# Log-sum-exp of 16,384 rows: one row's exponentials on GpSimd as powers of e, summed on VectorE ahead of the fifth load

## The chip, the cores and the metric

The kernel runs on one core of a Trainium2 chip. The metric is the device time of one execution in microseconds (us). Three runs of the kernel before the change gave 162.43, 162.54 and 162.83 us. One further execution was taken with the hardware profiler.

The core's engines work at the same time and wait for each other by semaphores. ScalarE (ACT in the profile) computes exponentials and logarithms, VectorE (DVE) sums, GpSimd (POOL) so far sets a few constants, TensorE (PE) does one tiny product at the end. SyncE (SP) issues the transfers, which 16 DMA engines carry out.

## The reference

The input is 32 x 512 rows of 1024 float32 numbers, 67.1 MB; of each row the logarithm of the sum of its exponentials is wanted.

```python
def reference(x, axis):
    x_max = np.max(x, axis=axis, keepdims=True)
    return (x_max.squeeze(axis) + np.log(np.sum(np.exp(x - x_max), axis=axis))).astype(np.float32)
```

## The kernel before

Each of the 128 partitions owns 128 rows that follow each other in memory, so "one row" below means one row in every partition: 128 x 1024 numbers, 0.52 MB. The kernel does not subtract the maximum. It takes exp(x) directly, sums, takes the logarithm, and then tests that all the sums lie between 1e-18 and 1e18. If they don't, a second pass (lines 189 to 201 and 322 to 343) reads everything again and subtracts the maxima. With the numbers at hand the first pass suffices.

The rows come in 17 loads, the list `CHUNKS` (line 10). An entry has the rows of the load, how many of them VectorE sums, in how many parts those are worked, and whether VectorE sums "by halves". The loads have 4, 15, 16, 16, 16, 14, 13, 9, 7, 5, 4, 3, 2, 1, 1, 1, 1 rows. They go into a ring of 51 row slots in the on-chip memory (`ring`, line 75); lines 118 to 125 give each load its slots one behind the other, and start again at slot 0 where a load doesn't fit any more.

Per load the code (lines 213 to 270) does this:

- SyncE issues the load (line 155), once the sums and exponentials of the rows that lay in its slots before are done. `busy` (line 128) holds for each slot the number of VectorE's or ScalarE's instruction to wait for. SyncE issues in order: a load that waits holds up the loads behind it. The first load is moved ahead of the opening barrier (lines 352 to 360).
- ScalarE waits for the landing (line 233) and writes the exponentials over the rows, one instruction for each part (line 235). For a load of `(16, 15, 2, False)` the parts have 8 and 7 rows; `cuts` (line 131) gives the first part the larger half.
- VectorE waits for each part (line 239) and sums its rows: one reduction for the part (line 255), or, by halves, one instruction a row that adds the row's halves and accumulates (line 242, with a read of the accumulator behind it).
- The rows beyond the second number of the entry are left to ScalarE alone: exponential and sum in one instruction (line 262, with a read of the accumulator behind it).

Everything on an engine runs in the order of the code. The logarithms are on ScalarE: of the first 81 rows ahead of the eighth load (line 219), of the next 43 ahead of the last load's exponential (line 221), of the last four at the end (line 272). The second of these waits for VectorE's sums of the thirteenth load, and the last row's exponential (line 225) is queued behind it. Then VectorE takes the largest and smallest of 124 sums (lines 293 and 294), compares with the bounds (line 283, twice), TensorE counts (lines 304 and 307), VectorE sums the counts (line 312), and the engines branch on the result.

GpSimd's only work is to set the bounds and the weights of that count (lines 206 to 209); the last of its settings raises `pool_done`, for which VectorE waits at line 298.

Of the kernel before, what the change touches and what calls it, by code (L numbers as in the profile page):

```python
# [1 line left out]

# [5 lines left out]


CHUNKS = [  # L10
# [4 lines left out]
]  # L15

CUTS = ()
RING_ROWS = 51


UNEVEN = ()
# [17 lines left out]
def kernel(  # L39
# [6 lines left out]
    nc = tc.nc  # L46
    P = nc.NUM_PARTITIONS
# [4 lines left out]
    N, D = x_flat.shape  # L52
# [5 lines left out]
    fp32, bf16, int32 = mybir.dt.float32, mybir.dt.bfloat16, mybir.dt.int32  # L58
    Exp = mybir.ActivationFunctionType.Exp
    Ln = mybir.ActivationFunctionType.Ln  # L60
    Alu = mybir.AluOpType
    AX = mybir.AxisListType.X
# [11 lines left out]

    ring = nc.alloc_sbuf_tensor("ring", [P, RING_ROWS, D], fp32).ap()
    sums = nc.alloc_sbuf_tensor("sums", [P, NB], fp32).ap()
# [4 lines left out]
    weights = nc.alloc_sbuf_tensor("weights", [P, 2], bf16).ap()  # L81
    verdict = nc.alloc_sbuf_tensor("verdict", [1, 1], int32).ap()
    peak = nc.alloc_sbuf_tensor("peak", [P, NB], fp32).ap()
    votes = nc.alloc_psum_tensor("votes", [P, 512], fp32).ap()
    late = nc.alloc_psum_tensor("late", [P, 512], fp32).ap()

# [4 lines left out]
    landed = [nc.alloc_semaphore(f"landed{i}") for i in range(len(CHUNKS) + len(spans) - 1)]  # L91
    act_done = nc.alloc_semaphore("act_done")
    dve_done = nc.alloc_semaphore("dve_done")
    pool_done = nc.alloc_semaphore("pool_done")
# [20 lines left out]
    symbolic, nc._always_lower_symbolic_ap = nc._always_lower_symbolic_ap, False  # L115


    place = []
    row = slot = 0
    for r, *_ in CHUNKS:  # L120
        if slot + r > RING_ROWS:
            slot = 0
        place.append((slot, row))
        slot += r
        row += r


    busy = [(0, 0)] * RING_ROWS
    acts = dves = 0

    def cuts(n, parts):
        ends = [-(-n * k // parts) for k in range(parts + 1)]
        return [(lo, hi) for lo, hi in zip(ends, ends[1:]) if lo < hi]

    def load(i):
        (s, row), r = place[i], CHUNKS[i][0]
        act_wait = max(a for a, _ in busy[s : s + r])
        dve_wait = max(d for _, d in busy[s : s + r])
        if dve_wait:
            nc.sync.wait_ge(dve_done, dve_wait)  # L140
        if act_wait:
            nc.sync.wait_ge(act_done, act_wait)
        dst, src = ring[:, s : s + r], x_v[:, row : row + r]
        if i == len(CHUNKS) - 1:
            for k, (lo, hi) in enumerate(spans):
                nc.sync.dma_start(out=dst[:, :, lo:hi], in_=src[:, :, lo:hi]).then_inc(
                    landed[i + k], 16
                )
        elif i in UNEVEN:
            for first, last, step in PARTS:  # L150
                nc.sync.dma_start(
                    out=dst[first:last:step], in_=src[first:last:step]
                ).then_inc(landed[i], 16)
        else:
            nc.sync.dma_start(out=dst, in_=src).then_inc(landed[i], 16)

    def take_logs(lo, hi, src, dve_wait, act_wait, bias=0.0):
        nonlocal acts
        nc.scalar.wait_ge(act_done, act_wait)
        if dve_wait:  # L160
            nc.scalar.wait_ge(dve_done, dve_wait)
        nc.scalar.activation(out=res[:, lo:hi], in_=src, func=Ln, bias=bias).then_inc(  # L162
            act_done, 1
        )
        acts += 1
# [4 lines left out]
    def total(t):  # L170
        return late[:, t - late_row : t - late_row + 1] if t >= late_row else sums[:, t : t + 1]
# [17 lines left out]
    with nc.body("second_vector", valid_engines=vector):  # L189
        for k, (lo, hi) in enumerate(steps):  # L190
# [5 lines left out]
                out=part, in0=part, in1=peak[:, lo:hi].unsqueeze(2).to_broadcast([P, hi - lo, D])  # L196
# [6 lines left out]
    nc.switch_bb("first_pass")  # L203

    nc.scalar.preload_act_table_set("natural_log_exp_and_others")  # L205
    nc.gpsimd.memset(bounds[:, 0], LOW)  # L206
    nc.gpsimd.memset(bounds[:, 1], HIGH)  # L207
    nc.gpsimd.memset(weights[:, :1], 1.0)
    nc.gpsimd.memset(weights[:, 1:], -TOO_MANY).then_inc(pool_done, 1)

    logged = 0
    done_before = [(0, 0)]
    for i, (r, n_dve, parts, by_halves) in enumerate(CHUNKS):
        if i:
            load(i)
        s, row = place[i]
        if i == LN_AT:
            logged = place[i - LN_LAG][1]
            take_logs(0, logged, sums[:, :logged], *done_before[i - LN_LAG])
        if i == len(CHUNKS) - 1:  # L220
            take_logs(logged, late_row, sums[:, logged:late_row], *done_before[-LATE])
            early_logs = acts
            for k, (lo, hi) in enumerate(spans):
                nc.scalar.wait_ge(landed[i + k], 16)
                nc.scalar.activation(  # L225
                    out=ring[:, s, lo:hi],
                    in_=ring[:, s, lo:hi],
                    func=Exp,
                    accum_out=late[:, LATE - 1 + k : LATE + k],
                ).then_inc(act_done, 1)  # L230
                acts += 1
            continue
        nc.scalar.wait_ge(landed[i], 16 * (len(PARTS) if i in UNEVEN else 1))
        for lo, hi in cuts(n_dve, parts):
            nc.scalar.activation(  # L235
                out=ring[:, s + lo : s + hi], in_=ring[:, s + lo : s + hi], func=Exp
            ).then_inc(act_done, 1)
            acts += 1
            nc.vector.wait_ge(act_done, acts)
            if by_halves:  # L240
                for j in range(lo, hi):
                    nc.vector.tensor_tensor_reduce(  # L242
                        out=ring[:, s + j, : D // 2],
                        in0=ring[:, s + j, : D // 2],
                        in1=ring[:, s + j, D // 2 :],
                        scale=1.0,
                        scalar=0.0,
                        op0=Alu.add,
                        op1=Alu.add,
                        accum_out=sums[:, row + j : row + j + 1],  # L250
                    ).then_inc(dve_done, 1)
                    dves += 1
                    busy[s + j] = (0, dves)
            else:
                nc.vector.reduce_sum(  # L255
                    out=sums[:, row + lo : row + hi], in_=ring[:, s + lo : s + hi], axis=AX
                ).then_inc(dve_done, 1)
                dves += 1
                for j in range(lo, hi):
                    busy[s + j] = (0, dves)  # L260
        for j in range(n_dve, r):
            nc.scalar.activation(  # L262
                out=ring[:, s + j],
                in_=ring[:, s + j],
                func=Exp,
                accum_out=total(row + j),
            ).then_inc(act_done, 1)
            acts += 1
            busy[s + j] = (acts, 0)
        done_before.append((dves, acts))  # L270
# [10 lines left out]
    def compare(lo, hi, values):  # L281
# [13 lines left out]
        out=ends[:, 1:], in_=sums[:, :late_row], axis=AX, op=Alu.min  # L295
    ).then_inc(dve_done, 1)
    dves += 2
    nc.vector.wait_ge(pool_done, 1)
    nc.vector.wait_ge(dve_done, dves)
    compare(0, 2, ends)  # L300
    nc.vector.wait_ge(act_done, acts)
# [20 lines left out]
    with nc.body("second_pass", valid_engines=[*vector, *others]):  # L322
        for k, (lo, hi) in enumerate(steps):
            if k:
                nc.sync.wait_ge(dve_again, 3 * k)
            for a, b in pieces(lo, hi):
                nc.sync.dma_start(
                    out=ring[:, a - lo : b - lo], in_=x_v[:, a:b]
# [67 lines left out]
```

## Time and profile before

| | us |
|---|---|
| median of three runs | 162.54 |
| the profiled execution | 162.67 |
| its span, first to last instruction | 161.3 |
| VectorE busy (51 instructions) | 121.9 |
| ScalarE busy (40 instructions) | 115.1 |
| GpSimd busy (8 instructions) | 0.4 |
| DMA engines' share of the span in input transfers | 97.4% |

The span is 1.4 us shorter than the profiled execution's time; what lies around it is not in the profile. "Busy" adds up the instructions of an engine. In the profile's lists of groups a row reads: source line, engine, operation, tiles written and read, shapes (partitions x numbers), count, then total busy time, mean of one in ns, the engine's idle time just ahead, and what ended it. In a list by time a row reads: start, duration (both in us), engine, line, operation, tiles and shapes, and in brackets the idle time ahead and what ended it.

### The profile page before, as it was taken

What the parts mean: (1) busy time and instruction counts of PE and PEld (TensorE: products, weight loads), DVE (VectorE), ACT (ScalarE), POOL (GpSimd) and SP (SyncE); (2) the same over time, 40 slices, a digit from 0 to 9 for tenths busy, and PEclk for the clock granted to TensorE, in tenths of its full rate; (3) what the DMA queues carried; (4) which work ended last, traced back from release to release, by engine and by line L of the source; (5) the groups of instructions that cost most, each with busy time, mean ns of one, the idle gap of its engine ahead of it and who ended that gap; (6) DMA issues with size and microseconds to landing.
All of it is one profiled execution on the core that took longest, in us unless ns stands there. A gap on an engine that the chain in (4) does not pass through costs nothing.

```text
span 161.3 us, 149 instructions
## 1 busy us (share of the span) xinstructions
PE 0.2 (0%) x2; PEld 0.1 (0%) x2; DVE 121.9 (76%) x51; ACT 115.1 (71%) x40; POOL 0.4 (0%) x8
## 2 busy tenths in 40 slices
PE   0000000000000000000000000000000000000000
PEld 0000000000000000000000000000000000000000
DVE  0028000003999999999999699999999999999884
ACT  3170005996079960999419993999199999999996
POOL 1000000000000000000000000000000000000000
DMA  7999799979979989989979999999999999999991
GB/s 256 508 488 442 305 472 520 439 341 520 439 341 520 423 358 520 423 358 520 423 325 455 455 455 439 423 423 423 412 402 430 436 420 410 427 436 412 417 407 42
DMA packets 2737, 67.18 MB, mean 417 GB/s; under 512 B 560, under 2 KB 560, under 8 KB 1072
## 3 DMA queue, kind: packets, MB, share of 16 engines
q1 hardware_dynamic: 2736, 67.18, 97.4%
q14 instruction: 1, 0.01, 0.0%
HBM read 67.11 MB, written 0.07 MB: 416 GB/s over the span
## 4 chain that ended last, share of the span: by engine, by line
DMA 49%; DVE 30%; ACT 20%; issue 0%; PE 0%
DMA ring<-in_x_dram 49%; DVE sums L255 29%; ACT ring L235 17%; ACT ring L262 3%; ACT ring L225 1%; ACT res L162 0%; DVE above L283 0%; PE votes L304 0%; DVE verdict L312 0%; PE votes L307 0%
## 5 line engine op out<-in xcount | busy, mean ns | idle before, releaser
L255 DVE TENSOR_REDUCE sums<-ring 128x8 f32<-128x8192 f32 (+5 forms) x14 | 111.2, 7994 | 37.3 <-ACT ring L235 37.2
L235 ACT ACTIVATE ring<-ring 128x8192 f32<-128x8192 f32 (+6 forms) x18 | 104.4, 5836 | 43.9 <-DMA ring<-in_x_dram 43.9
L242 DVE CUSTOM_DVE_ANT_0 ring<-ring 128x512 f32<-128x512 f32 x16 | 9.9, 684 | 0.0
L262 ACT ACTIVATE ring<-ring 128x1024 f32<-128x1024 f32 x8 | 8.2, 1041 | 0.0
L205 ACT ACT_TABLE_LOAD x1 | 1.3, 1283 | 0.8 <-PEq L377 0.8
L262 ACT ACTIVATION_READ_ACCUMULATOR ring<-ring 128x1 f32 x8 | 1.4, 174 | 0.0
L242 DVE DVE_READ_ACCUMULATOR2_ANT sums<- 128x1 f32 x16 | 1.3, 80 | 0.0
L225 ACT ACTIVATE ring<-ring 128x1024 f32<-128x1024 f32 x1 | 1.0, 1040 | 0.0
L283 DVE TENSOR_TENSOR above<-late,bounds 128x8 bf16<-128x8 f32 x1 | 0.2, 168 | 0.7 <-ACT res L162 0.7
L162 ACT ACTIVATE res<-sums 128x81 f32<-128x81 f32 (+1 forms) x2 | 0.5, 248 | 0.0
L312 DVE TENSOR_REDUCE verdict<-votes 1x1 int32<-1x6 f32 x1 | 0.2, 152 | 0.3 <-PE votes L307 0.3
L293 DVE TENSOR_REDUCE ends<-sums 128x1 f32<-128x124 f32 x1 | 0.3, 282 | 0.1
L304 PE MATMUL votes<-above,weights 128*1 128x6 bf16 x1 | 0.2, 167 | 160.0 <-DVE above L283 160.0
L294 DVE TENSOR_REDUCE ends<-sums 128x1 f32<-128x124 f32 x1 | 0.3, 271 | 0.0
L283 DVE TENSOR_TENSOR above<-ends,bounds 128x4 bf16<-128x4 f32 x1 | 0.2, 162 | 0.1
L162 ACT ACTIVATE res<-late 128x4 f32<-128x4 f32 x1 | 0.2, 173 | 0.0
L304 PEld LDWEIGHTS votes<-above,weights 128*1 128x1 bf16 x1 | 0.1, 80 | 160.0 <-DVE above L283 160.0
L307 PE MATMUL votes<-above,weights 128*1 128x6 bf16 x1 | 0.2, 165 | 0.0
L225 ACT ACTIVATION_READ_ACCUMULATOR ring<-ring 128x1 f32 x1 | 0.2, 153 | 0.0
L206 POOL MEMSET bounds<- 128x6 f32 x1 | 0.1, 104 | 0.4 <-POOLq L377 0.4
L207 POOL MEMSET bounds<- 128x6 f32 x1 | 0.1, 104 | 0.0
L377 POOL MEMSET const-bfloat16-1.0<- 128x1 bf16 x1 | 0.1, 103 | 0.0
(6 smaller groups left out, 0.6 us busy)
## 6 DMA issues: line engine op xcount, KB each, us to landing
ring<-in_x_dram SPq DMA_DIRECT2D x1, 7680.0 KB, 25.1
ring<-in_x_dram SPq DMA_DIRECT2D x1, 7168.0 KB, 28.6
ring<-in_x_dram SPq DMA_DIRECT2D x1, 6656.0 KB, 35.7
ring<-in_x_dram SPq DMA_DIRECT2D x1, 4608.0 KB, 20.3
ring<-in_x_dram SPq DMA_DIRECT2D x2, 2048.0 KB, 16.2
ring<-in_x_dram SPq DMA_DIRECT2D x1, 3584.0 KB, 28.5
ring<-in_x_dram SPq DMA_DIRECT2D x1, 2560.0 KB, 27.5
ring<-in_x_dram SPq DMA_DIRECT2D x4, 512.0 KB, 27.2
```

The source lines that it names most:

```text
L162: nc.scalar.activation(out=res[:, lo:hi], in_=src, func=Ln, bias=bias).then_inc(act_done, 1)
L205: nc.scalar.preload_act_table_set("natural_log_exp_and_others")
L225: nc.scalar.activation(out=ring[:, s, lo:hi], in_=ring[:, s, lo:hi], func=Exp, accum_out=late[:, LATE - 1 + k : LATE + k],).then_inc(act_d ...
L235: nc.scalar.activation(out=ring[:, s + lo : s + hi], in_=ring[:, s + lo : s + hi], func=Exp).then_inc(act_done, 1)
L242: nc.vector.tensor_tensor_reduce(out=ring[:, s + j, : D // 2], in0=ring[:, s + j, : D // 2], in1=ring[:, s + j, D // 2 :], scale=1.0, scal ...
L255: nc.vector.reduce_sum(out=sums[:, row + lo : row + hi], in_=ring[:, s + lo : s + hi], axis=AX).then_inc(dve_done, 1)
L262: nc.scalar.activation(out=ring[:, s + j], in_=ring[:, s + j], func=Exp, accum_out=total(row + j),).then_inc(act_done, 1)
L283: nc.vector.tensor_tensor(out=above[:, :, lo:hi], in0=values.unsqueeze(1).to_broadcast([P, 2, hi - lo]), in1=bounds[:, :, lo:hi], op=Alu.i ...
L293: nc.vector.reduce_max(out=ends[:, :1], in_=sums[:, :late_row], axis=AX).then_inc(dve_done, 1)
L294: nc.vector.tensor_reduce(out=ends[:, 1:], in_=sums[:, :late_row], axis=AX, op=Alu.min).then_inc(dve_done, 1)
L304: nc.tensor.matmul(votes[:1, :K], lhsT=weights[:, :1], rhs=above[:, 0], start=True, stop=False)
L307: nc.tensor.matmul(votes[:1, :K], lhsT=weights[:, 1:], rhs=above[:, 1], start=False, stop=True).then_inc(counted, 1)
```

## The change

The first load is still four rows, but the last of them no longer goes to ScalarE. GpSimd waits for the first load and then computes e to the power of x for this row, in place, with one element-wise instruction whose first operand is a column `base` that holds e, spread over 1024 numbers. VectorE sums this row by an instruction of its own, `POWER_AT = 4`, that is ahead of the fifth load's sums and waits for GpSimd.

So that GpSimd may take its time, the row's slot is kept for it: the first load goes to the ring's last four slots (47 to 50), the next three loads leave these four free, and the later loads leave slot 50 free. The fifth load has 15 rows instead of 16 (14 of them for VectorE, in parts of 7 and 7, one for ScalarE alone as before), the sixth 15 instead of 14 (all for VectorE, in parts of 8 and 7 instead of 7 and 7). VectorE's wait for GpSimd ahead of the comparison goes.

In the built program GpSimd gets two instructions more beside the setting of `base` and its waits: the power, and ahead of it one that reloads an instruction library and that carries the power's line.

```diff
 CHUNKS = [
-    (4, 4, 1, False), (15, 15, 1, False), (16, 16, 2, False), (16, 16, 2, False),
-    (16, 15, 2, False), (14, 14, 2, False), (13, 12, 2, False), (9, 8, 1, False),
+    (4, 3, 1, False), (15, 15, 1, False), (16, 16, 2, False), (16, 16, 2, False),
+    (15, 14, 2, False), (15, 15, 2, False), (13, 12, 2, False), (9, 8, 1, False),
...
+POWER_AT = 4
...
+    base = nc.alloc_sbuf_tensor("base", [P, 1], fp32).ap()
...
-    place = []
-    row = slot = 0
-    for r, *_ in CHUNKS:
-        if slot + r > RING_ROWS:
+    place = [(RING_ROWS - CHUNKS[0][0], 0)]
+    row, slot = CHUNKS[0][0], 0
+    for k, (r, *_) in enumerate(CHUNKS[1:]):
+        if slot + r > RING_ROWS - (CHUNKS[0][0] if k < 3 else 1):
             slot = 0
...
+    power_slot, power_row = place[0][0] + CHUNKS[0][0] - 1, CHUNKS[0][0] - 1
+    assert power_slot == RING_ROWS - 1
+    nc.gpsimd.memset(base, math.e)
     nc.gpsimd.memset(bounds[:, 0], LOW)
     nc.gpsimd.memset(bounds[:, 1], HIGH)
     nc.gpsimd.memset(weights[:, :1], 1.0)
     nc.gpsimd.memset(weights[:, 1:], -TOO_MANY).then_inc(pool_done, 1)
+    nc.gpsimd.wait_ge(pool_done, 1)
+    nc.gpsimd.wait_ge(landed[0], 16)
+    nc.gpsimd.tensor_tensor(
+        out=ring[:, power_slot],
+        in0=base.to_broadcast([P, D]),
+        in1=ring[:, power_slot],
+        op=Alu.pow,
+    ).then_inc(pool_done, 1)
...
         nc.scalar.wait_ge(landed[i], 16 * (len(PARTS) if i in UNEVEN else 1))
+        if i == POWER_AT:
+            nc.vector.wait_ge(pool_done, 2)
+            nc.vector.reduce_sum(
+                out=sums[:, power_row : power_row + 1], in_=ring[:, power_slot], axis=AX
+            ).then_inc(dve_done, 1)
+            dves += 1
         for lo, hi in cuts(n_dve, parts):
...
-        for j in range(n_dve, r):
+        for j in range(n_dve, r if i else 0):
...
-    nc.vector.wait_ge(pool_done, 1)
```

More of the change, by code (lines that the diff above doesn't have):

```diff
@@ L1 @@
+import math
 from contextlib import ExitStack
```

## The prediction, made before the changed kernel ran

> **What bounds the kernel now.** I read the page's header and its 40 slices first, then the busy time in the stretches between landings, then the groups by shape, then the order of time on ScalarE and VectorE at the end. The header and the DMA row say that the DMA engines are nearly full until the last slice.
>
> ```profile
> span 161.3 us, 149 instructions
> DMA  7999799979979989989979999999999999999991
> HBM read 67.11 MB, written 0.07 MB: 416 GB/s over the span
> ```
>
> The stretches below run from one load's landing to the next (us; PE, PEld, VectorE, ScalarE, POOL busy; clock, DMA share, GB/s). The times are those of the landing semaphores; where ScalarE waited, it starts 0.02 behind.
>
> ```profile
> 45.20:64.57 19.37, 0.00 (x0) 0.00 (x0) 19.37 (x3) 13.95 (x2) 0.00 (x0) 1.00 1.00 433
> 83.90:100.86 16.96, 0.00 (x0) 0.00 (x0) 15.40 (x3) 14.13 (x4) 0.00 (x0) 1.00 0.99 429
> 100.86:116.59 15.73, 0.00 (x0) 0.00 (x0) 15.73 (x3) 12.24 (x2) 0.00 (x0) 1.00 0.97 417
> 147.17:158.41 11.24, 0.00 (x0) 0.00 (x0) 10.00 (x24) 11.22 (x12) 0.00 (x0) 1.00 0.91 377
> ```
>
> Sixteen rows take 19.37 us, 14 take 16.96, 13 take 15.73: 1.21 us a row whatever the size. The chain of waits shows pieces such as "122.29 24.89 DMA", but a load issued then stands in a queue behind others; the stream never stops, and the last load lands at 158.41 us. VectorE is just as full: from 38.91 it has one idle time of 1.56 us (ended at 90.99, by the exponentials of the fifth load) and one of 1.13 us (ended at 153.68). The groups give the prices.
>
> ```profile
> L255 DVE TENSOR_REDUCE sums<-ring 128x8 f32<-128x8192 f32 x6 | 51.8, 8679 | 1.7 <-ACT ring L235 1.6
> L235 ACT ACTIVATE ring<-ring 128x8192 f32<-128x8192 f32 x6 | 41.9, 7022 | 17.2 <-DMA ring<-in_x_dram 17.2
> L235 ACT ACTIVATE ring<-ring 128x7168 f32<-128x7168 f32 x4 | 24.6, 6168 | 2.8 <-DMA ring<-in_x_dram 2.8
> L255 DVE TENSOR_REDUCE sums<-ring 128x7 f32<-128x7168 f32 x3 | 22.7, 7610 | 0.0
> ```
>
> At the end three things tie, in order of time:
>
> ```profile
> 147.19 2.76 ACT L235 ACTIVATE ring<-ring 128x3072 f32<-128x3072 f32 x1 [0.23 <-DMA ring<-in_x_dram]
> ...
> 153.68 3.35 DVE L255 TENSOR_REDUCE sums<-ring 128x3 f32<-128x3072 f32 x1 [1.13 <-ACT ring L235]
> ...
> 158.17 0.08 DVE L242 DVE_READ_ACCUMULATOR2_ANT sums<- 128x1 f32 x1
> 158.30 0.16 ACT L262 ACTIVATION_READ_ACCUMULATOR ring<-ring 128x1 f32 x1
> 158.35 0.24 ACT L162 ACTIVATE res<-sums 128x43 f32<-128x43 f32 x1
> ...
> 158.49 1.04 ACT L225 ACTIVATE ring<-ring 128x1024 f32<-128x1024 f32 x1
> ```
>
> The second logarithm (158.35) stands on ScalarE ahead of the last exponential (158.49) and waits for VectorE's sums of the thirteenth load, done at 158.25. ScalarE's own queue allows it at 158.35 (0.05 after the accumulator read at 158.30), and the last landing would allow the exponential at about 158.44. So a gain anywhere can't bring the end forward by more than about 0.05 us, while VectorE late by more than about 0.05 us pushes the end out one for one. Only the 1.13 us before 153.68 shields it.
>
> **The change part by part.** *First load, 3 rows on ScalarE.* Its exponentials fall from 3.62 us (4096 elements) to 2.76 (3072), its sums from 4.42 to 3.35. Both engines then idle anyway until 25.88 and 38.91 (14.72 and 23.30 us): worth 0.
>
> *New slots.* The first load moves to slots 47 to 50, and each later load's waits with it. The issue of load 5 of 17 still waits for the 15-row sum (55.06), load 6 for the second half of the third load (72.25). Load 7 now needs the second half of the fourth (89.43 instead of 80.84), loads 9 and 10 the first half of the sixth (about 116.5 instead of 107.2 and 114.7), loads 11 to 13 its second (about 124.1 instead of 122.3), the last four the first half of the seventh (about 130.5 instead of 128.7). Their bytes are due on the engines at about 100.9, 127.5, 142.3 and 153.3, so 11 us or more stay in hand each time: 0. The queue order on SyncE is the same.
>
> *Loads of 16 and 14 rows become 15 and 15.* The fifth lands one row, 1.21 us, earlier, near 82.7; the sixth at the same 100.86, as 30 rows are 30 rows. From there on every landing stays.
>
> *The power on GpSimd and its wait.* VectorE waits for it behind the fourth load's sums, at 89.43; queued behind are all its later sums, and behind those SyncE's loads and the two logarithms. The trace has no such operation. The nearest rows: one row's exponential on ScalarE takes 1.04 us; on GpSimd a memset of 6 elements takes 0.104 us, at most 17 ns an element, 1024 of them 17.8 us. From the landing at 7.53 to 89.43 there are 82 us, 80 ns an element, nearly five times that. No row bounds a power from above; I take it as hidden, being nearest to the memset row in engine, and keep "late" as a rival. The Trainium skill ("GPSIMD Engine Reference", Performance versus the Vector engine) gives 4497 ns for an addition of 2048 floats there; half of it, 2.2 us, as an estimate, would be done by 10 us and leave the sum as it is, but the page prices no power, and no run here shows one yet.
>
> *The instruction that the build puts ahead of the power on GpSimd* (it bears the power's line and reloads a library). Low end 0: GpSimd would wait for the first load until 7.53 anyway. High end: its bytes share the DMA engines; the only row is one 8 KB instruction fetch near 159.5 us, 0.61 us on one engine, and four such on one engine would hold every later landing 2.4 us. I take 0, since all fetches but that one lie outside the stream in this trace, and keep 2.4 for the range.
>
> *VectorE from 89.43 on.* Start-to-start, a sum of 8 rows takes 8.60 (90.99 to 99.60), of 7 rows 7.53 (99.60 to 107.12), of 6 rows 6.46: 1.07 a row and 0.07 each, so the new one-row sum takes 1.14. It ends at 90.6, in what was the 1.56 us of idleness; the fifth load's first half (now 7 rows, exponentials 82.7 + 6.17 = 88.9) is ready. Two sums of 7 end at 90.6 + 7.53 + 7.53 = 105.6. Now the sixth load: its first half has 8 rows instead of 7, and they land at 100.86 as before, so their exponentials end at 100.88 + 7.03 = 107.91 instead of 107.05. VectorE idles 2.2 us where it had no gap, starts at 107.94 instead of 107.12, and now has 15 rows instead of 14 behind it. The seventh load's sums start at 107.94 + 8.60 + 7.53 = 124.06 instead of 122.18: 1.88 late. Before, the eighth load's sum waited 0.2 us at 135.30 for its exponentials; that wait goes, 1.68 remain. The half-row sums that end at 152.55 end at 154.2, past the 153.65 at which the next exponentials are ready: of the 1.68 the gap of 1.13 absorbs all but 0.55, less 0.05 as the sum starts back to back. So the thirteenth load's sums end near 158.77, the logarithm moves by 0.5 and the last exponential too. The removed wait on GpSimd lay where VectorE idles 0.73 us: 0.
>
> *Sum.* 0 + 0 + 0 + 0 (bounds 0 and 2.4) + 0.52: the profiled execution, 162.67 us (span 161.3 and 1.4 around it), would take 163.2. It stands 0.13 above the median of 162.54, so the median comes to 163.05, 0.3% more. A measurement of this kernel tells about 0.3% (0.49 us) from no change, so this stands on the edge.
>
> **The rivals.** *The power is late.* It costs nothing while it ends by 91.6: the 2.2 us gap takes that up. Beyond, each us costs one, as VectorE's chain runs unbroken from the sixth load to the end. An end at 100 us gives 171.5; 93 gives 164.5. For it: the page shows GpSimd doing nothing but memsets, so nothing says how fast it takes powers. Against: 80 ns an element is long.
>
> *Not slower: the delay is absorbed.* If VectorE's catch-up from 107.94 to 153.7 were 0.5 us shorter than I add up, the tail would tie as it does now, 162.55. It decides at the 153.65 of the exponentials. Against it: the durations repeat to 0.01 us (8,675 to 8,685 ns for 8 rows).
>
> *The library's bytes or a fetch in the stream.* One packet of 0.61 us on one engine gives 163.65, four give 165.5.
>
> *GpSimd and VectorE exclude each other.* Then a power of 40 us costs what it holds of VectorE's full stretch: 7.6 + 40 = 47.6, less 38.91, less the 2.2 us gap, 6.5 us: 169.5. Up to 33 us it costs nothing. Nothing in this profile overlaps the two. "SBUF — State Buffer" of the Trainium skill (Who interferes with whom) says that a VectorE reduction never contends on this chip, while "Perfetto Trace Analysis" (Optimizing Scalar/DVE Operations) warns that moving work between the two may not help as they share a read port; no run here shows which holds.
>
> *The powers come out beyond the bounds of the verdict.* Then the second pass reads everything again: 155 us of loads more, over 318 us. The bounds are 1e-18 and 1e18; one chance in a hundred.
>
> **How the numbers follow.** My forecast (up to 0.75 us more) 0.58; power late 0.17; extra bytes over 0.6 us 0.07; exclusion 0.03; absorbed 0.08; second pass 0.01; faster for a reason that I don't see 0.05; the last 0.01 left with no change. Of the forecast's share a little over half, 0.34, lies above 0.49 us, the rest within. Slower: 0.34 + 0.17 + 0.07 + 0.03 + 0.01 = 0.62. Within 0.3%: 0.24 + 0.08 + 0.01 = 0.33. Faster: 0.05. The range goes from 162.4 (absorbed, less the spread of the median) to 165.5 (four packets, or a power that ends by 94); most of the late power, the exclusion and the second pass lie above, under 0.2 together. The forecast's own range is 162.9 to 163.3.
>
> **What would show it.** On VectorE a one-row sum near 89.4 with no wait ahead of it; a new idle time of about 2.2 us that ends near 107.9 by ScalarE's exponentials; no idle time near 153.7, the three-row sum starting at 154.2; the second logarithm at about 158.9 released by VectorE, the last exponential at 159.0. Landings as before from 100.9 on, the last at 158.4. Wrong if the power ends after 91.6, if a landing moves, or if sums beside the power take longer than 8.68 us.

## The result and the profile after

The changed kernel takes 242.2 us (four runs, 242.16 to 242.35) against 162.6 us before (four runs): 1.491 times as long, 95% interval 1.489 to 1.494. The forecast was 163.05 us, with a range up to 165.5. What happened is the rival "the power is late", and far later than the range allowed for.

From the page of the changed kernel: header, the busy tenths of four rows of 40 slices (6.0 us each), and the chain that ended last.

```profile
span 240.9 us, 154 instructions
DVE  0220005999999980000000000000699999999996
ACT  2400794597399299299692000000000002999972
POOL 0799999999999999999999999999300000000000
DMA  8998989898979989999000000000000799999930
...
POOL 68%; DVE 28%; DMA 3%; ACT 1%; issue 0%; PE 0%; ACTq 0%; POOLq 0%
```

Before, the DMA row was full to the end. Now there is a hole in the middle in which only GpSimd works: VectorE stops at 89.2 us, the DMA engines run out of work at 116.5 and ScalarE at 128.0, and all three start again only after GpSimd has ended. The groups name the two instructions (last columns: total busy us, mean ns; idle time ahead, its releaser).

```profile
L221 POOL TENSOR_TENSOR ring<-base,ring 128x1024 f32<-128x1024 f32 x1 | 163.2, 163219 | 6.6 <-DMA ring<-in_x_dram 6.6
...
L253 DVE TENSOR_REDUCE sums<-ring 128x1 f32<-128x1024 f32 x1 | 1.2, 1219 | 81.7 <-POOL ring L221 81.7
```

The power takes 163.2 us, as long as the whole kernel before. It starts at 7.62, as soon as the first load is there, and ends at 170.84; VectorE has waited for it for 81.7 us. What stands behind VectorE shows in order of time, first on VectorE, then on ScalarE (start, duration, then in brackets the idle time ahead).

```profile
71.91 17.27 DVE L278 TENSOR_REDUCE sums<-ring 128x8 f32<-128x8192 f32 x2
170.87 1.22 DVE L253 TENSOR_REDUCE sums<-ring 128x1 f32<-128x1024 f32 x1 [81.69 <-POOL ring L221]
172.01 52.77 DVE L278 TENSOR_REDUCE sums<-ring 128x7 f32<-128x7168 f32 x7
```

```profile
127.86 0.19 ACT L285 ACTIVATION_READ_ACCUMULATOR ring<-ring 128x1 f32 x1
203.37 0.27 ACT L167 ACTIVATE res<-sums 128x81 f32<-128x81 f32 x1 [75.32 <-DVE sums L278]
```

ScalarE gets as far as the seventh load and then stands in front of the first logarithm, which needs sums that VectorE hasn't made. The eighth load needs slots that VectorE hasn't read: SyncE issues it at 187.17 us, where it was 107.23 before. So one late row stopped three engines.

The stretches (VectorE is the third pair, ScalarE the fourth, POOL the fifth) show the bookkeeping:

```profile
7.50:89.20 81.70, 0.00 (x0) 0.00 (x0) 53.88 (x6) 50.23 (x8) 81.58 (x1) 1.00 1.01 434
89.20:170.80 81.60, 0.00 (x0) 0.00 (x0) 0.00 (x0) 31.38 (x9) 81.60 (x1) 1.00 0.30 132
170.80:237.90 67.10, 0.00 (x0) 0.00 (x0) 66.96 (x41) 29.99 (x19) 0.04 (x1) 1.00 0.64 266
```

And of the kernel before, the two stretches of the same work:

```profile
7.50:89.40 81.90, 0.00 (x0) 0.00 (x0) 54.91 (x6) 49.99 (x7) 0.00 (x0) 1.00 1.00 432
89.40:158.30 68.90, 0.00 (x0) 0.00 (x0) 66.04 (x41) 62.37 (x29) 0.00 (x0) 1.00 0.98 416
```

The first stretch is that of the kernel before to 0.2 us. The second is empty on VectorE. In the third VectorE is busy without a gap for 67.0 us and is itself the bound, the DMA engines only 64% busy. The kernel before needed 68.9 us for the same part, with its idle times in it. So the loss is 81.6 - (68.9 - 67.1) = 79.8 us: the span grew by 79.6.

### The profile page after: what moved, and what is told of

It is laid out like the page before. It is cut to its first block, busy times and chain, and to the rows that moved or that the text cites. A ratio compares the mean times of both kernels' runs of the same rounds, so it can differ in the third digit from the quotient of the medians.

```text
span 240.9 us, 154 instructions
## 1 busy us (share of the span) xinstructions
PE 0.2 (0%) x2; PEld 0.1 (0%) x2; DVE 121.9 (51%) x52; ACT 114.3 (47%) x40; POOL 163.7 (68%) x10
## 3 DMA queue, kind: packets, MB, share of 16 engines
q1 hardware_dynamic: 2736, 67.18, 65.4%
## 4 chain that ended last, share of the span: by engine, by line
POOL 68%; DVE 28%; DMA 3%; ACT 1%; issue 0%; PE 0%; ACTq 0%; POOLq 0%
POOL ring L221 68%; DVE sums L278 23%; DVE ring L265 4%; DMA ring<-in_x_dram 3%; DVE sums L253 1%; ACT ring L242 0%; ACT res L167 0%; DVE above L306 0%; PE votes L326 0%; DVE verdict L334 0%; DVE sums L265 0%; PE votes L329 0%; ACTq L166 0%; POOLq L220 0%
## 5 line engine op out<-in xcount | busy, mean ns | idle before, releaser
L221 POOL TENSOR_TENSOR ring<-base,ring 128x1024 f32<-128x1024 f32 x1 | 163.2, 163219 | 6.6 <-DMA ring<-in_x_dram 6.6
L278 DVE TENSOR_REDUCE sums<-ring 128x8 f32<-128x8192 f32 (+4 forms) x14 | 110.0, 7916 | 35.3 <-ACT ring L258 35.3
L253 DVE TENSOR_REDUCE sums<-ring 128x1 f32<-128x1024 f32 x1 | 1.2, 1219 | 81.7 <-POOL ring L221 81.7
```

What stands on the lines that cost most here:

```text
L221: nc.gpsimd.tensor_tensor(out=ring[:, power_slot], in0=base.to_broadcast([P, D]), in1=ring[:, power_slot], op=Alu.pow,).then_inc(pool_done, 1)
L253: nc.vector.reduce_sum(out=sums[:, power_row : power_row + 1], in_=ring[:, power_slot], axis=AX).then_inc(dve_done, 1)
L278: nc.vector.reduce_sum(out=sums[:, row + lo : row + hi], in_=ring[:, s + lo : s + hi], axis=AX).then_inc(dve_done, 1)
```

## The experiments

The theory after the result: the time is 163.05 us while the power ends by 91.6, and one us more for each us beyond. The rivals: something else in the change costs time (the library reload, GpSimd beside VectorE, the wait itself); the 163 us are paid once and not by the element; the 0.5 us that the forecast added for the split into 15 and 15 rows are a miscount. Ratios are to the kernel before on the same chip, with 95% intervals.

### A cheap operation in the power's place

```diff
-        op=Alu.pow,
+        op=Alu.add,
```

The row then holds x + e, so this kernel leaves out its exponentials.

> GpSimd adds e to the row instead of raising e to it, with the same instruction form, the same library reload, the same wait; so the first load's last row holds no exponentials and its result is another. Theory A (the time comes from how long the power runs, and from nothing else of the change): VectorE finds the row ready at 89.2 us, the one-row sum takes 1.2 us, and what is left is the 0.5 us that the prediction worked out: 163.05 us. Rival B (the library reload, GpSimd's reading beside VectorE, or the wait itself costs time): well above 163.5, up to 242. Rival C (the 0.5 us were miscounted): 162.6.

Measured: 163.03 us, ratio 1.0043 (1.0027 to 1.0059). The page's group, and VectorE around the sixth load:

```profile
L221 POOL TENSOR_TENSOR ring<-base,ring 128x1024 f32<-128x1024 f32 x1 | 1.9, 1891 | 6.4 <-DMA ring<-in_x_dram 6.4
```

```profile
88.97 1.21 DVE L253 TENSOR_REDUCE sums<-ring 128x1 f32<-128x1024 f32 x1
90.09 15.14 DVE L278 TENSOR_REDUCE sums<-ring 128x7 f32<-128x7168 f32 x2
107.54 22.67 DVE L278 TENSOR_REDUCE sums<-ring 128x8 f32<-128x8192 f32 x3 [2.31 <-ACT ring L258]
```

The same instruction on the same numbers takes 1.89 us instead of 163.2: the operation is the price. The reload, the wait and the new slots are all still in this kernel, and of the 79.6 us nothing is left but the 0.6 us that the split alone costs (below). The gap of 2.2 us that the prediction put ahead of the sixth load's sums is there with 2.31.

### Half of the power, and five eighths

GpSimd takes the last 512 or 640 numbers of the row, ScalarE the rest:

```diff
+POWER_COLS = 512
...
     nc.gpsimd.tensor_tensor(
-        out=ring[:, power_slot],
-        in0=base.to_broadcast([P, D]),
-        in1=ring[:, power_slot],
+        out=ring[:, power_slot, D - POWER_COLS :],
+        in0=base.to_broadcast([P, POWER_COLS]),
+        in1=ring[:, power_slot, D - POWER_COLS :],
...
+        if i == 0:
+            nc.scalar.activation(
+                out=ring[:, power_slot, : D - POWER_COLS],
+                in_=ring[:, power_slot, : D - POWER_COLS],
+                func=Exp,
+            ).then_inc(act_done, 1)
+            acts += 1
```

> GpSimd takes the power of 512 of the row's 1024 numbers, ScalarE the exponentials of the other 512 right behind the first load's three rows. Theory A, with a price by the element (163.2 us for 1024, so 159 ns each): the power ends at 7.6 + 81.6 = 89.2 us, ahead of the 91.6 from which it costs anything: 163.05 us. Rival D (most of the 163 us is paid once, for example for loading code): the power still takes well over 100 us and the kernel well over 180.

> As the run with 512 numbers, with 640 on GpSimd and 384 on ScalarE. Theory A: the power takes 102.0 us, ends at 109.6, which is 18.0 past the 91.6, and each of these costs one: 181.1 us. Rival D: over 200. If part of VectorE's lateness were made up later, less than 181.

Measured: 162.89 us with 512 numbers, ratio 1.0032 (1.0020 to 1.0044); 181.31 us with 640, ratio 1.1165 (1.1141 to 1.1189). First the run with 512, its group and then VectorE's wait.

```profile
L222 POOL TENSOR_TENSOR ring<-base,ring 128x512 f32<-128x512 f32 x1 | 81.9, 81927 | 6.6 <-DMA ring<-in_x_dram 6.6
```

```profile
89.55 1.22 DVE L254 TENSOR_REDUCE sums<-ring 128x1 f32<-128x1024 f32 x1 [0.39 <-POOL ring L222]
```

And the same of the run with 640:

```profile
L222 POOL TENSOR_TENSOR ring<-base,ring 128x640 f32<-128x640 f32 x1 | 102.3, 102338 | 6.5 <-DMA ring<-in_x_dram 6.5
```

```profile
109.91 1.22 DVE L254 TENSOR_REDUCE sums<-ring 128x1 f32<-128x1024 f32 x1 [20.80 <-POOL ring L222]
```

Between 512 and 640 numbers the power grows by 20.41 us, 159 ns a number; from 512 to 1024 by 81.29, 159 again. Carried back to zero numbers, these slopes leave 0.3 and 0.6 us that could be paid once. And the threshold is where the prediction had it, to some 0.2 us: with 512 VectorE even waits 0.39 us for the power and the time is that of the kernel with the cheap addition; with 640 the power ends at 109.88, 18.3 past 91.6, and the time is 181.31 - 162.89 = 18.4 above. From there to 1024 the power ends 60.96 us later and the time grows by 242.2 - 181.3 = 60.9.

### The wait moved to the end

The full power, but VectorE's wait and sum behind all other sums; the first four rows get a logarithm of their own at the end:

```diff
-            take_logs(0, logged, sums[:, :logged], *done_before[i - LN_LAG])
+            take_logs(4, logged, sums[:, 4:logged], *done_before[i - LN_LAG])
...
-        if i == POWER_AT:
-            nc.vector.wait_ge(pool_done, 2)
...
     take_logs(late_row, NB, late[:, : NB - late_row], dves, acts)
+    nc.vector.wait_ge(pool_done, 2)
+    nc.vector.reduce_sum(
+        out=sums[:, power_row : power_row + 1], in_=ring[:, power_slot], axis=AX
+    ).then_inc(dve_done, 1)
+    dves += 1
+    take_logs(0, 4, sums[:, :4], dves, acts)
...
-    nc.sync.wait_ge(act_done, early_logs)
+    nc.sync.wait_ge(act_done, acts)
```

> The changed kernel with its full power of 1024 numbers; VectorE's wait and one-row sum stand behind all other sums instead of ahead of the fifth load's, the first logarithm leaves out the first four rows, and a fourth logarithm takes them at the end; the two stores wait for it. Theory A (the power's length costs by what is queued behind the wait): all other work is done by about 160 us while the power runs, it ends at 170.8, the one-row sum at 172.1, and some 3.6 us of comparison and branch follow: 175.7 us. If the power held up other engines' work by running, or cost the 79.6 us wherever it is waited for: well above 180, up to 242.

Measured: 176.76 us, ratio 1.0878 (1.0858 to 1.0897). GpSimd's group, then VectorE at its end:

```profile
L221 POOL TENSOR_TENSOR ring<-base,ring 128x1024 f32<-128x1024 f32 x1 | 163.2, 163219 | 6.5 <-DMA ring<-in_x_dram 6.5
```

```profile
158.00 0.69 DVE L259 CUSTOM_DVE_ANT_0 ring<-ring 128x512 f32<-128x512 f32 x1
170.81 1.22 DVE L291 TENSOR_REDUCE sums<-ring 128x1 f32<-128x1024 f32 x1 [12.12 <-POOL ring L221]
```

GpSimd's instruction is the same 163.2 us, and 65.4 of the 79.6 us are gone: VectorE's other sums were done at 158.7 and ScalarE's other work at 160.2, beside the power. So its running holds up nobody, and its price is set by what stands behind the wait. The miss of 1.1 us is for the most part in the ending: both stores are now issued behind the last logarithm (172.36 and 172.75), and SyncE waits 0.9 us for them, a wait that the kernel before doesn't have. No place in the code hides the full row: the power can't start before the first load is there, and it ends 9.5 us after the whole span of the kernel before.

### The split into 15 and 15 alone

In the kernel before, without a power:

```diff
-    (16, 15, 2, False), (14, 14, 2, False), (13, 12, 2, False), (9, 8, 1, False),
+    (15, 14, 2, False), (15, 15, 2, False), (13, 12, 2, False), (9, 8, 1, False),
```

> The kernel before with one edit: the fifth and sixth load as (15, 14, 2) and (15, 15, 2), no power, no GpSimd. Theory A: VectorE ends the fifth load's sums near 104.5, waits for the sixth load's first 8 rows until 107.9, and ends 0.5 us later than before: 163.05 us. Rival C (the delay is absorbed): 162.6 us.

Measured: 162.97 us, ratio 1.0035 (1.0021 to 1.0049), 0.57 us on the 162.4 of the kernel before on that chip. VectorE around the sixth load and at the end, and ScalarE's second logarithm:

```profile
80.65 23.73 DVE L255 TENSOR_REDUCE sums<-ring 128x8 f32<-128x8192 f32 x3
107.82 22.67 DVE L255 TENSOR_REDUCE sums<-ring 128x8 f32<-128x8192 f32 x3 [3.44 <-ACT ring L235]
...
154.04 3.35 DVE L255 TENSOR_REDUCE sums<-ring 128x3 f32<-128x3072 f32 x1
```

```profile
158.69 0.24 ACT L162 ACTIVATE res<-sums 128x43 f32<-128x43 f32 x1 [0.51 <-DVE sums L242]
```

VectorE is done at 104.38, waits until 107.82, has no idle time left ahead of the three-row sum, and the logarithm that ScalarE could start in its own time now stands 0.51 us for VectorE.

### Seven rows first

The sixth load's parts as 7 and 8 rows instead of 8 and 7; the same edit in the kernel with half the power, and in the split alone:

```diff
-        ends = [-(-n * k // parts) for k in range(parts + 1)]
+        ends = [n * k // parts for k in range(parts + 1)]
```

> As the run with 512 numbers, and the sixth load's two parts are 7 and 8 rows instead of 8 and 7. Theory A (the 0.5 us left come from the 8-row first part, whose exponentials end 0.86 us later): the part's sums start at 107.1 as in the kernel before, the extra row behind costs VectorE 1.07 us, of which the 0.2 us ahead of the eighth load's sum and the 1.13 us gap at the end take up all: 162.4 us, ratio to before 1.000. Rival E (the 0.5 us come from the extra row itself or from the power): 162.9 as before.

> The kernel before with the fifth and sixth load as (15, 14, 2) and (15, 15, 2), and the sixth load's parts as 7 and 8 rows. No GpSimd. Theory A: 162.4 us, ratio 1.000, since the sixth load's sums start at 107.1 as in the kernel before. Rival E: 162.9.

Measured: 162.49 us, ratio 0.9996 (0.9986 to 1.0005), with half the power; 162.54 us, ratio 1.0006 (0.9994 to 1.0017), for the split alone. VectorE in the run of the split alone:

```profile
107.01 22.67 DVE L255 TENSOR_REDUCE sums<-ring 128x7 f32<-128x7168 f32 x3 [2.60 <-ACT ring L235]
...
153.44 3.35 DVE L255 TENSOR_REDUCE sums<-ring 128x3 f32<-128x3072 f32 x1
```

And ScalarE's second logarithm there, now with no idle time ahead:

```profile
158.11 0.24 ACT L162 ACTIVATE res<-sums 128x43 f32<-128x43 f32 x1
```

The sums start 0.8 us sooner and the logarithm no longer waits for VectorE: the whole 0.5 us hung on which part came first. The run with half the power also shows what GpSimd's half row is worth here: ScalarE has half a row less to do, the new slots and the reload are in, and the time is that of the kernel before. GpSimd spends 81.9 us on what ScalarE, at 1.04 us a row, does in 0.5, and ScalarE idles behind the first load anyway.

## Why the prediction was wrong

- *What bounds the kernel.* Right as far as the runs test it: 0.5 us of lateness on VectorE come out as 0.5 us, as the tie at the second logarithm said. That a gain could not bring the end forward is not shown: the half row taken from ScalarE brings nothing (ratio 0.9996), but it came out of ScalarE's idle time behind the first load.
- *First load, new slots.* Right with 0, to the noise: the kernel with the cheap addition has both and takes 163.03 us, the split alone 162.97.
- *The split.* Right: 0.52 us forecast, 0.57 measured (0.34 to 0.80 by the interval), with the gap, the three-row sum without idle time and the logarithm released by VectorE all there, within 0.5 us of where they were put.
- *The library reload.* Right with 0: the trace has it as two entries of 11 ns near 1.0 us, and the kernel with the cheap addition, which holds it, takes no longer than the split alone. Of the packets that were feared in the stream the trace shows none: inside the span the queue of instruction fetches has one of 8 KB, as in the kernel before, and both stand behind the last load.
- *The power.* This step failed: "I take it as hidden, being nearest to the memset row in engine". The memset row gave at most 17 ns a number, 17.8 us a row; the power takes 159 ns a number, 163.2 us, nine times as much and twice the 82 us at hand. The row was near in engine and far in work: a memset computes nothing, and no row of the trace showed GpSimd computing. The prediction said that no row bounds it from above and still gave lateness 0.17 and a range that ended at a power done by 94. The page of the Trainium skill that it weighed beside that ("GPSIMD Engine Reference", Performance versus the Vector engine) would have misled in the same way: it prices an addition and no power. The addition of the row measured 1.89 us, where the estimate from the page was 2.2; the power costs 86 times the addition.
- *The rival "the power is late".* Its price was right to 0.1 us: 163.05 + (170.84 - 91.6) = 242.3, measured 242.2. Threshold and slope are confirmed by the runs with 512 and 640 numbers. Only its chance and the end of the range were wrong.
- *GpSimd and VectorE excluding each other.* Not so here: VectorE's sums of 8 rows take 8,677 ns in the run with the wait at the end, where all six stand beside the power, and 8,679 before. This agrees with the Trainium skill, "SBUF — State Buffer" (Who interferes with whom), that a reduction on VectorE doesn't contend. The warning in the Trainium skill's "Perfetto Trace Analysis" (Optimizing Scalar/DVE Operations) doesn't bite for this pair of instructions.

## What to carry to other kernels

An operation that the trace doesn't show on an engine has no price from a neighbour that does another kind of work: if no row bounds it from above, work out the time it has, and keep a large chance for its not fitting, or measure it alone first. What a slow instruction costs is set by the first in-order queue that waits for it and by how much of the kernel stands behind; a wait in the middle of VectorE's sums stopped SyncE's loads and ScalarE as well. And where one engine works in parts behind another, the size of the first part is the gap: 8 rows first cost 0.5 us, 7 rows first nothing.

## What the runs showed of the hardware

On GpSimd an element-wise power of float32 took 159 ns a number in each partition (81.9 us for 512, 102.3 for 640, 163.2 for 1024). It took the same 163,219 ns where VectorE idled beside it for 81.7 us (the changed kernel) and where VectorE worked beside it up to 158.7 us (the wait at the end). An addition in the same form took 1.85 ns a number (1.89 us for 1024). Why a power costs so much more, no run here shows.
